# A hybrid encoder block on one core: the last token pair of the feed-forward's second half takes all its weights in one visit

## The chip, the core and the metric

The kernel runs on one core of a Trainium2 chip. A core has a matrix engine (TensorE, PE in the profile, with its weight loads shown apart as PEld), a vector engine (VectorE, DVE), a scalar engine (ScalarE, ACT), a general engine (GpSimd, POOL) and a queue that issues transfers (SyncE, SP). Data lie in SBUF; matmuls accumulate in eight PSUM banks of 128 x 512 floats. The metric is the time of one execution in device microseconds; a comparison uses the median of several.

## The reference

One layer of an encoder block, 2048 tokens and 16 meta tokens, width 1024, in float32:

```python
h = concatenate([meta, x], axis=1)
p = rms_norm(h, norm_mix_pre) @ w_in
mixed = concatenate([rg_lru(p), forgetting_attention(p), rwkv7(p)]) @ w_out
h = h + rms_norm(mixed, norm_mix_post)
f = causal_dwconv(rms_norm(h, norm_ffn_pre) @ ffn_up, ffn_conv)      # 1024 -> 2 x 2816
gate, val = split(f, 2)
f = (gelu(gate) * val) @ ffn_down                                    # 2816 -> 1024
h = h + rms_norm(f, norm_ffn_post)
return h[:, N_META:]
```

The change concerns the last four lines, above all `@ ffn_down` and the norm behind it, which end the kernel.

## The kernel before

**Numbers.** Every float32 operand of a matmul is split into a high part (`hi`, a copy on ACT, L1602) and a low part (`lo = x - hi`, on DVE, in places on POOL, L1603). One product is three matmuls, hi x hi, hi x lo and lo x hi (`mm3`, L172, L173, L174).

**The up stage** computes the first half of the feed-forward for blocks of 342 tokens in units j of the feature columns. It accumulates in banks `psu`. A unit's sums are combined on DVE, convolved (`conv`: an ACT scaling at L1736 into `uy` and two multiply-adds on DVE, L1738), put through the gelu and multiplied on POOL (L1744), and stored to the scratch `scr_ff` (L1745). Some units read their sum from an SBUF tile (`vb`), others straight from the PSUM bank.

**The down stage** (class `Down`) has 2048 tokens as eight token pairs of 256 tokens and 22 row blocks of `ffn_down`: ten weight pairs k = 0 to 9, and an eleventh, the rest. For each k a Strassen-like scheme takes seven products (`p1`, `p5`, `p7`, `p6`, `p2`, `p3`, `p4`) in place of eight, so 21 matmuls of 128 x 512. Its token operands come from `scr_ff` as `u` (256 KB, L1849), are summed by four POOL operations (L1856 to L1859) and split into `fo`. Its weight operands come as 256 KB loads `raw` (L1832) and are split into slots: nine kept ones (`qd`) and 26 of a ring (`dw`). Of the seven splits of a k, two have their low part on POOL, five on DVE. 35 slots hold five k. The rest is done without the scheme, 24 matmuls from weights `dwn`; three of its four sums share a bank with `p2`, `p3` and `p4`, the fourth has a bank `rb`.

As 35 slots do not hold ten k, the stage makes two rounds. `first` goes through the eight pairs with k = 0 to 4; each pair's seven banks are evacuated by ACT (L1888 to L1890) and DVE (L1891 to L1895, L1904) into four half rows `la`, `ra`, `lb`, `rb`, and stored to `scr_part`. Then `second` goes through the eight pairs with k = 5 to 9 and the rest; after the evacuation the stored part comes back (`pt`, 512 KB a row) and is added on POOL (L1901), the row is normalised (ACT squares L1516, the root L102 to L104, DVE L1525) and added to `h` (`hx`, loaded at L1920, L1526), and stored to the output (L1922). One pair has 105 matmuls in the first round and 129 in the second.

The operands of k = 0, and two of k = 1, are prepared in the last round of the up stage from unit j = 14 on (`DOWN_FROM`); the others follow when the down stage begins, the rest's weights with them. The operands of k = 5 to 9 are prepared when the last first visit no longer needs the slots of k = 0 to 4.

**What sets the order.** The kernel is written as one program; a scheduler puts it in an order for each engine, by dependences and due times. `issue_after(x)` keeps what is written in it behind x on the queues. Pools hand out buffers in turn (a tag has so many), and a tile waits until the last reader of its buffer is done. Each engine executes its own list in order.

## Time and profile before

| | us |
|---|---|
| median of 3 runs | 3065.51 (3058.34 to 3071.79) |
| the profiled execution | 3063.42 |
| its span | 3061.7 |
| last matmul of the up stage starts | 2592.17 |
| last matmul of the down stage starts | 3050.16 |

The mean granted clock of the profiled execution is 0.971. Times in a row are microseconds from the start of the span; `[3.57 <-DVE uy L1738]` behind a row says that the engine was idle for 3.57 us before it and that a DVE instruction of line 1738 that writes `uy` ended the idle time. In a table by stretches the numbers behind a stretch are its length, the busy time of each engine with the count of its instructions, the granted clock of PE, and the share and rate of the DMA engines. In a row of groups `xcount | busy, mean ns | idle before` stand for the number of instructions, their busy time in all and mean duration, and the idle time of the engine just before them with what ended it.

### The profile page before, as it was taken

Reading aid. Unit: us, or ns where it says so; the run is one execution under the profiler, and the core shown is the slowest. Engines: PE = TensorE matmul, PEld = TensorE weight load, DVE = VectorE, ACT = ScalarE, POOL = GpSimd, SP = SyncE. Lnnn points to the kernel's source line nnn. Section 1 sums busy time; section 2 is a strip of 40 time slices with the busy share of each in tenths; the row PEclk is TensorE's granted clock in tenths of the full one; section 3 lists DMA queues with packets and bytes.
Section 4 is the critical chain, followed back from the end, with each engine's and each line's share of the span. In section 5 each row is a group of like instructions: output and inputs, shape, how many; then the busy total and the mean of one; then the engine's idle time right before and its main releaser. Section 6 shows DMA issues by size and latency. Waiting matters only on the chain.

```text
span 3061.7 us, 52809 instructions
## 1 busy us (share of the span) xinstructions
PE 2910.2 (95%) x18694; PEld 2487.6 (81%) x18694; DVE 2057.7 (67%) x3934; ACT 1479.1 (48%) x2853; POOL 1365.7 (45%) x1599
## 2 busy tenths in 40 slices
PE   6998999999989999999999899999999999999998
PEld 6997898888876654566568899999999999787786
DVE  5268645656677785555636888888778777547766
ACT  4245332434346554454534656666566665324333
POOL 1001121122214556566843457445645544556765
PEclk8999999999989898999999999999999999999999
DMA  6776478466654347434336555566677765535454
GB/s 216 244 234 207 163 240 292 154 199 205 211 156 92 88 105 211 109 100 122 75 94 206 171 181 180 172 202 213 209 215 212 220 192 165 171 102 175 148 162 145
DMA packets 467750, 532.58 MB, mean 174 GB/s; under 512 B 85550, under 2 KB 355576, under 8 KB 465932
## 3 DMA queue, kind: packets, MB, share of 16 engines
q1 hardware_dynamic: 466716, 528.27, 56.5%
q8 instruction: 147, 2.41, 0.3%
q14 instruction: 119, 0.97, 0.1%
q0 software_dynamic: 768, 0.93, 0.1%
HBM read 369.11 MB, written 159.95 MB: 173 GB/s over the span
## 4 chain that ended last, share of the span: by engine, by line
PE 34%; DVE 5%; DMA 5%; POOL 3%; issue 3%; ACT 1%; SPq 0%; POOLq 0%; DVEq 0%; ACTq 0%
PE psu L172 8%; PE psu L173 8%; PE psu L174 8%; PE psd L172 2%; PE psd L173 2%; PE psd L174 2%; DMA u<-scr_ff 2%; DMA xt<-scr_h 1%; DVE uw L1603 1%; PE pswo L172 1%; PE pswo L174 1%; PE pswo L173 1%; DVE fo L1603 1%; DVE uy L1738 1%; POOL u L1858 1%
## 5 line engine op out<-in xcount | busy, mean ns | idle before, releaser
L172 PE MATMUL psu<-xo,uw 128*128 128x344 f32 x1848 | 590.8, 323 | 14.7 <-DVE vb L1787 6.9
L173 PE MATMUL psu<-xo,uw 128*128 128x344 f32 x1848 | 593.1, 321 | 0.0
L174 PE MATMUL psu<-xo,uw 128*128 128x344 f32 x1848 | 584.3, 320 | 1.5 <-DVE uw L1603 1.5
L172 PE MATMUL psp<-xh,wh 128*128 128x384 f32 (+2 forms) x1152 | 383.5, 333 | 4.5 <-ACT wh L166 3.0
L174 PE MATMUL psp<-xh,wl 128*128 128x384 f32 (+2 forms) x1152 | 379.5, 330 | 2.6 <-DMA wl<-scr_wk 2.5
L173 PE MATMUL psp<-xl,wh 128*128 128x384 f32 (+2 forms) x1152 | 379.3, 329 | 0.0
L1603 DVE TENSOR_TENSOR uw<-uq,uw 128x512 fp32r<-128x512 f32 x341 | 321.0, 947 | 65.1 <-ACT uw L1602 62.8
L172 PEld LDWEIGHTS psu<-xo,uw 128*128 128x128 f32 x1848 | 347.4, 189 | 19.2 <-DVE vb L1787 9.4
L174 PEld LDWEIGHTS psu<-xo,uw 128*128 128x128 f32 x1848 | 347.2, 189 | 2.4 <-DVE uw L1603 2.3
L173 PEld LDWEIGHTS psu<-xo,uw 128*128 128x128 f32 x1848 | 348.5, 189 | 0.1
L1602 ACT ACTIVATE uw<-uq 128x512 fp32r<-128x512 f32 x462 | 287.5, 627 | 107.5 <-PE psu L174 46.6
L686 ACT ACTIVATE p<-sc,bias 128x512 f32<-128x512 f32 (+4 forms) x352 | 197.0, 589 | 194.9 <-PE sc L682 162.1
L559 DVE TENSOR_REDUCE mc<-mx 128x1 f32<-128x512 f32 (+6 forms) x352 | 190.2, 564 | 114.1 <-PE mx L554 87.2
L1738 DVE SCALAR_TENSOR_TENSOR uy<-psu,ffn_cols,uy 128x342 f32<-128x342 f32 (+1 forms) x396 | 223.7, 567 | 62.3 <-ACT uy L1736 60.9
L1744 POOL TENSOR_TENSOR uy<-uy,uy 128x342 f32<-128x342 f32 (+1 forms) x132 | 140.0, 1061 | 252.7 <-DVE uy L1738 70.1
L725 POOL TENSOR_TENSOR acc<-acc,p 128x512 f32<-128x512 f32 (+3 forms) x208 | 221.7, 1068 | 53.1 <-DVE acc L725 23.9
L1603 POOL TENSOR_TENSOR uw<-uq,uw 128x512 fp32r<-128x512 f32 x121 | 177.6, 1468 | 148.0 <-ACT uw L1602 129.5
L172 PEld LDWEIGHTS psp<-xh,wh 128*128 128x128 f32 x1152 | 221.7, 192 | 11.6 <-issue 4.2
L174 PEld LDWEIGHTS psp<-xh,wl 128*128 128x128 f32 x1152 | 220.8, 192 | 12.0 <-issue 5.7
L173 PEld LDWEIGHTS psp<-xl,wh 128*128 128x128 f32 x1152 | 221.3, 192 | 7.5 <-issue 5.4
L1603 DVE TENSOR_TENSOR fo<-u,fo 128x896 fp32r<-128x896 f32 x88 | 109.0, 1240 | 118.8 <-ACT fo L1602 118.8
L1602 ACT ACTIVATE fo<-u 128x896 fp32r<-128x896 f32 x88 | 81.1, 922 | 200.9 <-POOL u L1859 103.8
(470 smaller groups left out, 6470.3 us busy)
## 6 DMA issues: line engine op xcount, KB each, us to landing
uq<-scr_us SPq DMA_DIRECT2D x220, 256.0 KB
uq<-in_ffn_up_dram SPq DMA_DIRECT2D x209, 256.0 KB
wl<-scr_wk SPq DMA_DIRECT2D x48, 512.0 KB
wh<-scr_wk SPq DMA_DIRECT2D x48, 512.0 KB
u<-scr_ff SPq DMA_DIRECT2D x88, 256.0 KB
scr_ff<-uy SPq DMA_DIRECT2D x110, 171.0 KB
raw<-in_w_in_dram SPq DMA_DIRECT2D x24, 512.0 KB
scr_wk<-wh SPq DMA_DIRECT2D x24, 512.0 KB
```

Source lines behind the costliest of these rows:

```text
L172: nc.tensor.matmul(out, ah, bh, start=first, stop=False, skip_group_check=more)
L173: nc.tensor.matmul(out, ah, bl, start=False, stop=False, skip_group_check=more)
L174: nc.tensor.matmul(out, al, bh, start=False, stop=last, skip_group_check=more)
L559: self.reduced = nc.vector.tensor_reduce(mc[:rows, i, ci : ci + 1], ps[:rows, : e - a], axis=AX.X, op=ALU.max)
L686: last = nc.scalar.activation(p[:rows, :w], ps[:rows, :w], AF.Exp, bias=bias[:rows, j : j + 1])
L725: eng.tensor_tensor(a, ps_[0][0][:rows, c0:n] if start and i == 1 else a, p[:rows, : n - c0], op=ALU.add)
L1602: core.nc.scalar.activation(hi, src, AF.Copy)
L1603: (eng or core.nc.vector).tensor_tensor(lo, src, hi, op=ALU.subtract)
L1738: stt(y[:, :n], src[:, i : n + i], cw[:, 44 * i + cc : 44 * i + cc + 1], y[:, :n], op0=ALU.mult, op1=ALU.add)
L1744: core.pooled = nc.gpsimd.tensor_tensor(v[:, :n], g[:, :n], v[:, :n], op=ALU.mult)
L1858: tt(s3, a0, b0, op=ALU.subtract)
```

## The change

- **The rounds.** `first` goes through seven pairs. The eighth takes k = 0 to 9 and the rest in one visit, stores no part, and is normalised and put out directly. `second` then goes through the other seven. The operands of k = 5 to 9 are written two k after the eighth pair's start (`ahead`, `DOWN_AHEAD`), behind its `u` loads, in one ring of 35 slots (25 `dw`, nine `qd` and a `kd` in the place of an earlier gain vector). The rest's weights are loaded and split in the fifth pair (`DOWN_REST`).
- **The stored parts.** They are loaded as four half rows of 256 KB (`fetch`, tag `dq`) in the visit before, and after the second k of a second visit (`DOWN_STORED`) three are added to the open banks of `p4`, `p2` and `p3` by DVE (L1924 of the changed kernel), while the fourth is copied to the `rb` bank by ACT. The matmuls that follow accumulate on top. The POOL additions of L1901 are gone.
- **The up stage's end.** The down operands begin at unit 13, three of k = 1 at unit 17. In the last unit the two sums that stayed in PSUM go to SBUF tiles (`u2`, `ga`), and a third bank is copied by ACT before its convolution. Splits of k = 2 and 3 are held behind the last convolution (`DOWN_HELD`, `ended`).
- **The end of a visit.** The rest goes in the order `p4`, `rb`, `p2`, `p3`, the evacuation in the order `lb`, `rb`, `la`, `ra`. `add_scaled` takes the place of `add_normed`: the half rows are multiplied by the gain (L1539) and then scaled and added in one DVE operation (L1543). Both `hx` rows are loaded together. In the last pair the products `p2`, `p3`, `p4` of k = 8 are kept to the end, and the output is stored by half rows.

The lines of the changed kernel are some 18 to 50 higher: the splits' L1603 is L1621 there, the side sums' L1856 to L1859 are L1886 to L1889, the evacuation's L1904 is L1948, and the convolution's L1738 is L1760.

Three places show how instructions move. First DVE at the end of the up stage, before: `uy` are the convolutions of the last unit, `dw` the low parts of down weights.

```order
L1790 TENSOR_TENSOR psu_28591<-psu_28591,ga_28525 128x344
L1603 TENSOR_TENSOR dw_28754<-raw_28752,dw_28754 128x512
L1603 TENSOR_TENSOR dw_28789<-raw_28787,dw_28789 128x512
L1603 TENSOR_TENSOR dw_28794<-raw_28792,dw_28794 128x512
L1738 SCALAR_TENSOR_TENSOR uy_28587<-vb_28540,ffn_cols,uy_28587 128x338
L1738 SCALAR_TENSOR_TENSOR uy_28605<-psu_28591,ffn_cols,uy_28605 128x342
L1738 SCALAR_TENSOR_TENSOR uy_28587<-vb_28540,ffn_cols,uy_28587 128x338
L1738 SCALAR_TENSOR_TENSOR uy_28624<-psu_28512,ffn_cols,uy_28624 128x342
```

The same place now:

```order
L1812 TENSOR_TENSOR vb_28553<-psu_28525,vb_28553 128x344
L1760 SCALAR_TENSOR_TENSOR uy_28600<-vb_28553,ffn_cols,uy_28600 128x338
L1760 SCALAR_TENSOR_TENSOR uy_28618<-ga_28538,ffn_cols,uy_28618 128x342
L1760 SCALAR_TENSOR_TENSOR uy_28600<-vb_28553,ffn_cols,uy_28600 128x338
L1760 SCALAR_TENSOR_TENSOR uy_28618<-ga_28538,ffn_cols,uy_28618 128x342
L1760 SCALAR_TENSOR_TENSOR uy_28639<-ga_28637,ffn_cols,uy_28639 128x342 x2
L1621 TENSOR_TENSOR dw_28748<-raw_28746,dw_28748 128x512
L1621 TENSOR_TENSOR dw_28753<-raw_28751,dw_28753 128x512
L1621 TENSOR_TENSOR fo_28793<-u_28787,fo_28793 128x896
```

The convolutions stand ahead of the splits, and read SBUF (`ga`, `vb`) where they read `psu`.

Second, POOL in the eighth pair, before: the four side sums of k = 3 end with the first row, those of k = 4 are `u_30183`.

```order
L1859 TENSOR_TENSOR u_30153<-u_30153 128x128
L1603 TENSOR_TENSOR qd_30233<-raw_30258,qd_30233 128x512
L1856 TENSOR_TENSOR u_30183<-u_30183 128x128
L1858 TENSOR_TENSOR u_30183<-u_30183 128x128
L1603 TENSOR_TENSOR qd_30233<-raw_30270,qd_30233 128x512
L1857 TENSOR_TENSOR u_30183<-u_30183 128x128
L1859 TENSOR_TENSOR u_30183<-u_30183 128x128
```

Now, with the side sums of k = 2 (`u_30141`) and k = 3 (`u_30199`):

```order
L1889 TENSOR_TENSOR u_30141<-u_30141 128x128
L1621 TENSOR_TENSOR qd_25384<-raw_30158,qd_25384 128x512
L1621 TENSOR_TENSOR qd_25384<-raw_30170,qd_25384 128x512
L1886 TENSOR_TENSOR u_30199<-u_30199 128x128
L1888 TENSOR_TENSOR u_30199<-u_30199 128x128
L1887 TENSOR_TENSOR u_30199<-u_30199 128x128
L1889 TENSOR_TENSOR u_30199<-u_30199 128x128
L1621 TENSOR_TENSOR kd_25385<-raw_30216,kd_25385 128x512
```

The first splits of the second five k stand one k earlier on POOL.

Third, DVE between two second visits, before, from the normalisation of one pair on; the `fo` are operands of the next pair.

```order
L1525 SCALAR_TENSOR_TENSOR ra_31315<-ra_31315,rs_5253_31338,g_fpost 128x512
L1603 TENSOR_TENSOR fo_31405<-u_31399,fo_31405 128x896
L102 TENSOR_SCALAR rs_5255_31351<-rs_5255_31351 128x1
L1526 TENSOR_TENSOR hx_31336<-hx_31336,la_31311 128x512
L1526 TENSOR_TENSOR hx_31336<-hx_31336,ra_31315 128x512
L104 RECIPROCAL rs_5255_31351<-rs_5255_31351 128x1
L1525 SCALAR_TENSOR_TENSOR lb_31313<-lb_31313,rs_5255_31351,g_fpost 128x512
L1525 SCALAR_TENSOR_TENSOR rb_31312<-rb_31312,rs_5255_31351,g_fpost 128x512
L1603 TENSOR_TENSOR fo_31435<-u_31429,fo_31435 128x896
L1526 TENSOR_TENSOR hx_31349<-hx_31349,lb_31313 128x512
L1526 TENSOR_TENSOR hx_31349<-hx_31349,rb_31312 128x512
L1603 TENSOR_TENSOR fo_31465<-u_31459,fo_31465 128x896
```

Now:

```order
L1543 SCALAR_TENSOR_TENSOR hx_30842<-lb_30827,rs_5183_30846,hx_30842 128x512
L1543 SCALAR_TENSOR_TENSOR hx_30842<-rb_30826,rs_5183_30846,hx_30842 128x512
L1621 TENSOR_TENSOR fo_30946<-u_30940,fo_30946 128x896
L104 RECIPROCAL rs_5184_30857<-rs_5184_30857 128x1
L1543 SCALAR_TENSOR_TENSOR hx_30844<-la_30825,rs_5184_30857,hx_30844 128x512
L1543 SCALAR_TENSOR_TENSOR hx_30844<-ra_30829,rs_5184_30857,hx_30844 128x512
L1924 TENSOR_TENSOR psd_30872<-psd_30872,pt_30762 128x512
L1924 TENSOR_TENSOR psd_30873<-psd_30873,pt_30764 128x512
L1924 TENSOR_TENSOR psd_30874<-psd_30874,pt_30758 128x512
L1621 TENSOR_TENSOR fo_30976<-u_30970,fo_30976 128x896
```

The additions into the open banks stand between the third and the fourth `fo` of the next pair, behind the whole normalisation of the last one.

The diff's core:

```diff
+def add_scaled(core, pool, halves, gain, x, junk):
...
+    for y, acc in zip(halves, sums):
+        nc.scalar.activation(junk, y, AF.Square, accum_out=acc)
+    for c, y in enumerate(halves):
+        nc.vector.tensor_tensor(y, y, gain[:, 512 * c : 512 * c + 512], op=ALU.mult)
+    r1 = rstd_root(core, v, sums, D)
+    for c, y in enumerate(halves):
+        xc = x[:, 512 * c : 512 * c + 512]
+        nc.vector.scalar_tensor_tensor(xc, y, r1, xc, op0=ALU.mult, op1=ALU.add)
+        yield xc
...
-DOWN_SLOTS = 5, 13, 8
-DOWN_FROM = 14
+DOWN_SLOTS = 5, 7, 1, 2, 10
+DOWN_FROM = 13, 17
+DOWN_HELD = 2, 4
+DOWN_AHEAD = 2
+DOWN_FETCH, DOWN_STORED = 2, 1
+DOWN_REST = 4
...
             elif name == "p3":
-                tt(ps, ps, u2, op=ALU.add)
-                gb = conv(ps, 0, j, n[1])
+                sum_ = ps if more else u2
+                tt(sum_, ps, u2, op=ALU.add)
+                gb = conv(sum_, 0, j, n[1])
...
-                va = conv(ps, 1, j, n[0])
+                src = ps
+                if not more:
+                    src = s("ga")
+                    nc.scalar.activation(src, ps, AF.Copy)
+                va = conv(src, 1, j, n[0])
...
+            products(k, side, slice(0, 4))
+            kept.append((k, side, slice(4, None)))
+            while kept and not (rest and following is None and k == ks[-2]):
+                products(*kept.pop(0))
+            if stored and i == DOWN_STORED:
+                for name, half in zip(("p4", "rb", "p2", "p3"), self.parts):
+                    if name == "rb":
+                        nc.scalar.activation(ps[name][:], half[:], AF.Copy)
+                    else:
+                        tt(ps[name][:], ps[name][:], half[:], op=ALU.add)
+            if following is not None and k == ks[-DOWN_FETCH]:
+                with core.tc.issue_after(self.loaded.ins):
+                    self.parts = self.fetch(following)
...
-        for i, row in enumerate(((lb, rb), (la, ra)) if rest else ()):
-            t0 = P * (2 * pair + i)
-            pt = self.spool.tile([P, D], F32, tag="hx", name=core.n("pt"))
-            nc.sync.dma_start(pt[:], self.scr["part"][t0 : t0 + P, :])
-            for c, y in enumerate(row):
-                nc.gpsimd.tensor_tensor(y, y, pt[:, 512 * c : 512 * c + 512], op=ALU.add)
-        for y, name in ((la, "p2"), (ra, "p3"), (lb, "p4"), (rb, "rb")):
+        for y, name in ((lb, "p4"), (rb, "rb"), (la, "p2"), (ra, "p3")):
...
+        steps.second(pairs - 1, range(DOWN_PAIRS), weights, ahead, rest, False, 0)
+        for pair in range(pairs - 1):
+            following = pair + 1 if pair < pairs - 2 else None
+            steps.second(pair, range(DOWN_CUT, DOWN_PAIRS), weights, lambda i: None, rest, True, following)
```

176 lines of the change are left out of this document (109 added, 67 removed).

## The prediction

> **What bounds the kernel now.** I read the share of the engines first, then a table of busy time in stretches around the feed-forward's second half, then PE's waits there, then the order of PE's instructions inside the two worst stretches. The columns of a stretch are its length, and busy us and count of PE, PEld, DVE, ACT and POOL, the granted clock, the DMA share and GB/s; the table of the psum tile `psd` alone has PE, PEld, DVE and ACT.
>
> ```profile
> PE 2910.2 (95%) x18694; PEld 2487.6 (81%) x18694; DVE 2057.7 (67%) x3934; ACT 1479.1 (48%) x2853; POOL 1365.7 (45%) x1599
> 2300.00:2570.00 270.00, 269.03 (x1702) 268.65 (x1701) 209.67 (x338) 166.72 (x336) 121.67 (x98) 1.00 0.67 197
> 2600.00:2630.00 30.00, 27.83 (x103) 20.63 (x103) 20.34 (x20) 17.73 (x28) 16.71 (x19) 0.91 0.75 257
> 2750.00:2780.00 30.00, 30.00 (x131) 24.46 (x130) 16.01 (x20) 7.30 (x9) 15.29 (x24) 1.00 0.32 108
> 2780.00:2810.00 30.00, 25.41 (x97) 19.43 (x96) 27.54 (x26) 21.96 (x37) 26.86 (x26) 0.89 0.75 245
> 2810.00:2840.00 30.00, 28.76 (x125) 23.13 (x124) 23.21 (x25) 10.34 (x17) 20.87 (x24) 0.99 0.40 130
> 2900.00:2930.00 30.00, 29.47 (x129) 23.72 (x128) 20.89 (x27) 9.96 (x19) 20.67 (x25) 1.00 0.49 158
> 3050.00:3062.00 12.00, 0.55 (x3) 0.12 (x1) 7.19 (x15) 2.97 (x10) 1.36 (x2) 0.61 0.36 134
> ```
> ```profile
> 2592.00:2600.00 8.00, 2.75 (x7) 1.67 (x8) 0.00 (x0) 0.00 (x0) 0.71 0.57 166
> ```
> ```profile
> L1888 ACT ACTIVATE la<-psd x5: 598/598/602, 2675.0 to 2771.6; 128x512 f32<-128x512 f32 x5
> L1888 ACT ACTIVATE la<-psd x7: 597/598/598, 2859.8 to 3042.3; 128x512 f32<-128x512 f32 x7
> ```
>
> PE is the bound, so the change is worth only the time that PE loses. The evacuation `la<-psd` comes once per token pair and is my pace-maker. Four intervals of the first visits give (2771.6-2675.0)/4 = 24.15 us for 105 matmuls, 0.230 us each. Against that pace a stretch is worth its length minus 0.230 us times its matmuls. The up stage (2300 to 2570) has PE busy 269 of 270 us. The steady first visits have 131 matmuls in 30 us, no loss. The losses are three, and a tail:
> - The step from up to down. After 2592.33 (row below) seven matmuls stand in the 7.67 us to 2600, a loss of 6.1, and 103 in the next 30 us, a loss of 6.3: together 12.4 us.
> - The step from first to second visits: 97 matmuls in 2780 to 2810 lose 7.7, 125 in the next 30 us lose 1.2: 8.9 us.
> - The second visits: six intervals give (3042.3-2859.8)/6 = 30.42 us for 129 matmuls, whose pace would be 29.67: 0.75 us per pair.
> - The tail from PE's last matmul to the end of the span.
>
> ```profile
> PE psd L172 <- ACT fo L1602: 6.1, 8, 2.8
> PE psd L172 <- DVE uy L1738: 4.9, 2, 3.6
> PE psd L174 <- DVE fo L1603: 3.7, 4, 1.3
> ```
> ```profile
> 2592.33 0.39 PE L172 MATMUL psd<-qd,fo 128*128 128x512 f32 x1
> 2596.76 0.77 PE L172 MATMUL psd<-qd,fo 128*128 128x512 f32 x1 [3.57 <-DVE uy L1738]
> 2599.72 0.76 PE L172 MATMUL psd<-qd,fo 128*128 128x512 f32 x1 [1.34 <-DVE uy L1738]
> 2602.42 0.63 PE L172 MATMUL psd<-qd,fo 128*128 128x512 f32 x1
> 2602.85 0.63 PE L173 MATMUL psd<-qd,fo 128*128 128x512 f32 x1
> ```
>
> The waits (total, times, longest) name what PE waited for: at the first step the last convolution `uy` on DVE, which still reads PSUM banks that the down stage wants; elsewhere the token operand `fo`. After the 3.57 us stop matmuls start 0.43 us apart (2602.42, 2602.85), about half pace, so a long stop is paid a second time.
>
> **The change, part by part.** All sums are against the profiled execution (3063.42 us, span 3061.7); it lies 2.1 us under the median 3065.51 of the three runs, so a gain is taken from the median in the end.
>
> (a) More first slots. Three more operands are split during the up stage, with their loads on SP, copies on ACT and subtractions on DVE or POOL. The last 270 us of the up stage leave DVE 60 us free and ACT 103, and PE never starves there: 0, with bounds 0 and 1 (one DVE split lying in PE's way).
>
> (b) The last up unit gives its PSUM up early: its sums go to SBUF, one copy on ACT replaces the convolution's direct read, and splits of k = 2 and 3 are held behind the last convolution. DVE runs the convolutions first (order rows in the section on the change). That removes the two waits on `uy`, 4.9 us, and with them the slow matmuls: in 2600 to 2612 there are about 4 us of those.
>
> ```profile
> 2600.00:2612.00 12.00, 11.14 (x34) 7.99 (x34) 0.00 (x0) 0.00 (x0) 0.77 0.87 306
> L1603 DVE TENSOR_TENSOR dw<-raw,dw 128x512 fp32r<-128x512 f32 x18 | 15.9, 923 | 3.1 <-ACT dw L1602 3.1
> L1603 DVE TENSOR_TENSOR fo<-u,fo 128x896 fp32r<-128x896 f32 x6 | 8.3, 1379 | 7.9 <-ACT fo L1602 7.9
> ```
>
> The 34 matmuls lose 12-34x0.230 = 4.2 us. What is late next is DVE: of each k's seven splits it does five, 5x0.923+1.379 = 6.0 us per k against PE's 21x0.230 = 4.83. Four operands of k = 1 and all of k = 2 to 4 are left, so DVE falls back 1.2 us for each of three k, about 3.5 us, while pair 1's work on k = 0 can fill some of it. The held splits wait behind the stores of the last `uy` on SP's and DVE's queues; behind them stand the `fo` of pair 0. Loss after: 3.5, with ends 1.5 (only the last k late) and 7 (all four k late and one slow spell). The loads and splits of the last two weight rows move from this place to the fifth pair, where a stretch like 2750 to 2780 has DVE free for 14 of 30 us: 0 there. I take 3.5, since the DVE rows give it: 12.4 becomes 3.5, -8.9, between -5.4 and -10.9.
>
> (c) The eighth pair takes ten k in one visit, in place of a first visit, its stores, a reload and a second visit. Its 35 splits for k = 5 to 9 go where the first-to-second step has them now, one k earlier in POOL's order. Here POOL decides, and it was busy 26.86 of 30 us:
>
> ```profile
> L1603 POOL TENSOR_TENSOR dw<-raw,dw 128x512 fp32r<-128x512 f32 x8 | 13.7, 1721 | 2.3 <-ACT dw L1602 2.3
> L1858 POOL TENSOR_TENSOR u<-u 128x128 f32<-128x128 f32 x7 | 7.1, 1013 | 0.0
> L1857 POOL TENSOR_TENSOR u<-u 128x128 f32<-128x128 f32 x7 | 5.4, 770 | 0.0
> L1859 POOL TENSOR_TENSOR u<-u 128x128 f32<-128x128 f32 x7 | 5.4, 769 | 0.5
> L1856 POOL TENSOR_TENSOR u<-u 128x128 f32<-128x128 f32 x7 | 5.0, 715 | 6.8 <-DMA u<-scr_ff 6.5 <-issue 0.3
> ```
>
> Per k: two splits 3.44 plus four side sums 3.27, 6.7 us against PE's 4.83. Over five k POOL falls back 9.4 us; it can be about one k (4.83) ahead when it begins. So PE still loses 9.4-4.8 = 4.6 us. Today it loses 8.9, with its evacuation and stores in the same stretch and a slow spell. The evacuation in the middle of that pair, its stores and their reload fall away. Now -4.3; ends +3 (POOL has no lead, and a slow spell of 2.5 us, less than the 4.2 of (b): 9.4+2.5 = 11.9 lost) and -7.
>
> (d) Stored parts in the second visits. The four POOL additions L1901 go; four loads of 256 KB stand behind a `u` load on SP; three DVE additions into open banks and one ACT copy come in, behind the second k of the next pair.
>
> ```profile
> L1901 POOL TENSOR_TENSOR la<-la,pt 128x512 f32<-128x512 f32 x4 | 7.0, 1740 | 0.0
> L1901 POOL TENSOR_TENSOR rb<-rb,pt 128x512 f32<-128x512 f32 x4 | 5.2, 1296 | 0.0
> L1856 POOL TENSOR_TENSOR u<-u 128x128 f32<-128x128 f32 x20 | 12.4, 622 | 37.8 <-DMA u<-scr_ff 33.6 <-DVE la L1525 3.2 <-DVE rb L1893 0.6
> L1602 ACT ACTIVATE fo<-u 128x896 fp32r<-128x896 f32 x20 | 19.0, 950 | 38.1 <-POOL u L1859 38.1
> L1784 DVE TENSOR_TENSOR psu<-psu,u 128x344 f32<-128x344 f32 x3 | 1.6, 518 | 1.3 <-PE psu L174 1.3
> L1904 DVE TENSOR_TENSOR la<-la,psd 128x512 f32<-128x512 f32 x5 | 3.4, 674 | 0.0
> L1526 DVE TENSOR_TENSOR hx<-hx,la 128x512 f32<-128x512 f32 x4 | 3.5, 882 | 0.0
> ```
> ```profile
> 3056.97 0.69 DVE L1526 TENSOR_TENSOR hx<-hx,rb 128x512 f32<-128x512 f32 x1
> ```
>
> Today POOL's side sums wait for L1525 behind the additions, `fo` waits for POOL, PE for `fo`: that is the 0.75 us per pair, and it goes. The price of the new addition is bounded by L1784, the one DVE addition into PSUM in this trace: 0.518 x 512/344 = 0.77 us, and from below by L1904, 0.67. I take 0.77, the same write. What may be late is DVE: from the last matmul of a pair it has eight evacuations and gain products (8x0.67), two `fo` (2x1.38), four scale-and-adds (4x0.69 as at 3056.97, or 4x0.88 beside POOL), and then the additions to p4 and p2 (2x0.77): 12.4 to 13.2 us, less one evacuation that it does before that matmul. PE comes to p2 of the third k after 2x4.83 plus 12 matmuls, 12.4 us. So it just fits or just doesn't; I put 0.3 us per pair, with ends 0 and 1.5 (0.88 for each of DVE's operations without PSUM, and the roots' small ones between them). Over seven pairs: 7x(0.3-0.75) = -3.2; ends -5.3 and +5.3.
>
> By the Trainium skill, page "GPSIMD Engine Reference", section "Key points", GpSimd's SBUF interfaces are contended by VectorE operations with two SBUF inputs. L1904 (one input from PSUM) against L1526 (two from SBUF) agrees, 674 and 882 ns; by the rule, with POOL's additions gone, DVE's two-input operations would come back toward 0.69, the 0.3 would be 0, and the sum 2.1 us lower.
>
> (e) The tail.
>
> ```profile
> 3050.16 0.39 PE L174 MATMUL psd<-dwn,fo 128*128 128x512 f32 x1
> 3054.95 3.07 SPq L1922 DMA_DIRECT2D out_dram<-hx  x2
> ```
>
> From 3050.55 to 3061.7 are 11.1 us: DVE to 3057.66, then the store of 512 KB, 4.0. The new normalisation multiplies by the gain before the sum of squares is there, so two DVE operations (1.4 us) leave the path, while the last stored half is 256 KB; POOL's additions leave it too, but DVE's order hides them. ACT's squares still come one after another. The other order of the rest's products and the products of k = 8 kept back in the last pair move matmuls without adding any: 0, since what follows on DVE is the same work in the same number of steps. I take -1.3, ends 0 and -2.
>
> Sum: 0-8.9-4.3-3.2-1.3 = -17.7 us. That is 3045.7 for the profiled execution, 3047.8 for the median: 3048.
>
> **Rivals.** First, the eighth pair stays as dear as the step it replaces (POOL 6.7 per k with no lead): (c) is +3 in place of -4.3 and the sum -10.4, 3055. For it: POOL's 26.86 of 30 us, and DVE's 27.54; against: the evacuation and stores that leave this stretch.
>
> Second, on the other side: the additions in open banks come late. `fo` of the fourth k stands behind them on DVE, and PE behind both. The place is p4 or p2 of the third k in each of seven pairs. For it: my sum has no slack; against: DVE is busy only 20.89 of 30 us. Its point: without (d)'s own gain the rest is -14.5 us, 2.1 per pair, so a stop of 2.1+0.75 us per pair brings the time back to 3065.5. A stop of 3.5 is followed by a slow spell as at 2596.76, which costs some 4.2: then 7x(3.5+4.2-0.75)-14.5 = +34, 3100; stops of 1.5, as bounded, give 3056. The Trainium skill ("TensorE: Matmul & The Clock Gate", part 1 on the HAM clock gate) puts the halving after about 3.4 us without work, in a window that runs freely. This trace agrees for the 3.57 us stop, but it also shows
>
> ```profile
> 2802.27 0.50 PE L172 MATMUL psd<-qd,fo 128*128 128x512 f32 x1 [2.81 <-ACT fo L1602]
> 2804.79 1.22 PE L174 MATMUL psd<-qd,fo 128*128 128x512 f32 x2 [1.31 <-DVE fo L1603]
> 2806.23 0.63 PE L173 MATMUL psd<-qd,fo 128*128 128x512 f32 x1
> ```
>
> where stops of 2.81 and 1.31 us close together were enough, so I price a stop from some 3 us on with a slow spell.
>
> Third, everything fits: (b) reaches -10.9, (c) -7, (d) -5.3, (e) -2, which is -25: 3040.
>
> **How the numbers follow.** The forecast has 0.52, the first rival 0.15, the second 0.18, the third 0.15. About 0.5% (15.3 us) is what a measurement of this kernel can tell from no change. The forecast's own range, 3041 to 3057, lies for four fifths below 3050.2: 0.43 faster and 0.09 same; the third rival is faster. The first rival is same. The second splits: 0.07 same (short stops), 0.11 slower than 3080.8. So faster 0.58, same 0.31, slower 0.11. The range 3036 to 3066 leaves out the second rival's long stops and the ends' far tails, less than 2 in 10.
>
> **What will show it.** (b): no wait of PE on `uy` over 1 us, no granted clock under 0.9 in the 20 us after the last up matmul, and some 140 matmuls or more in the 36 us after it. (c): the eighth pair's ten k in 53 us or less. (d): `la<-psd` of the second visits 30.0 us apart, and PE's waits on the additions under 0.5 us. (e): 9.8 us from PE's last matmul to the end. I am wrong if PE waits for DVE at p4 or p2 in each second visit, if POOL's lead in the eighth pair is gone, or if the up stage itself, which the change barely touches, gets longer.

## The result

The changed kernel takes 3044.18 us (median of six runs, 3038.31 to 3050.67), the kernel before 3063.36 us (median of six, 3058.34 to 3071.79): a ratio of 0.994, 95% interval 0.9928 to 0.9952, so 19.2 us or 0.6% faster. Ratios are of runs in the chip's fast state; the one slow run on record (4047.54 us at a granted clock of 0.641, of the kernel timed last below) is left out of them. The forecast was 3048 with a range of 3036 to 3066. The time was right; its parts were only partly right, and two of them for wrong reasons.

The profiled execution of the changed kernel has a span of 3042.5 us (3044.26 us in all), 19.2 us under that of the kernel before. The first question is where in the program these 19.2 us lie. The first matmul of the up stage tells (group of the matmuls `psu` of line 172, durations min/median/max, first and last start), first of the kernel before, then of the changed kernel:

```profile
L172 PE MATMUL psu<-xo,uw x1848: 314/321/656, 1682.0 to 2591.9; 128*128 128x344 f32 x185
```
```profile
L172 PE MATMUL psu<-xo,uw x1848: 315/321/653, 1675.0 to 2586.4; 128*128 128x344 f32 x185
```

7.0 us were won before the up stage begins, where both programs run the same instructions, in the same order but for a few matmuls that changed places. In the fourteen profiles of this study that start lies anywhere between 1674.5 and 1696.4 us: it is scatter. The up stage itself takes 909.9 and 911.4 us, from the first to the last start of these rows. What the change did is read from the down stage, from its first matmul to the end of the span: 469.4 us before, 455.6 now, -13.8 us. That measure is steady: a kernel that was profiled twice (below) gave 451.0 and 451.2. All comparisons below are made on it.

PE's stretches in the changed kernel (columns as before, the first number behind the stretch its length):

```profile
2590.00:2600.00 10.00, 9.17 (x39) 6.71 (x37) 6.08 (x7) 6.02 (x11) 4.02 (x4) 1.00 0.92 310
2600.00:2630.00 30.00, 26.96 (x105) 18.99 (x106) 23.58 (x26) 14.48 (x24) 22.49 (x26) 1.00 0.60 205
2850.00:2880.00 30.00, 30.00 (x132) 24.52 (x131) 20.47 (x31) 10.64 (x21) 12.47 (x21) 1.00 0.47 158
3030.00:3043.00 13.00, 3.03 (x14) 2.15 (x12) 8.57 (x17) 3.48 (x10) 0.00 (x0) 0.80 0.22 81
```

The pace-maker `la<-psd`, now line 1938, with the first matmul of the down stage ahead of it:

```profile
L172 PE MATMUL psd<-qd,fo x45: 390/394/502, 2586.9 to 2696.7; 128*128 128x512 f32 x45
```
```profile
L1938 ACT ACTIVATE la<-psd x2: 579/590/600, 2614.3 to 2639.8; 128x512 f32<-128x512 f32 x2
```
```profile
L1938 ACT ACTIVATE la<-psd x3: 598/599/601, 2760.6 to 2848.3; 128x512 f32<-128x512 f32 x3
```
```profile
L1938 ACT ACTIVATE la<-psd x7: 598/599/601, 2848.3 to 3026.2; 128x512 f32<-128x512 f32 x7
```

And PE's waits from 2560 us on:

```profile
PE psd L172 <- ACT fo L1620: 5.5, 3, 3.3
PE psd L173 <- DVE dw L1621: 1.8, 4, 0.7
PE psu L172 <- DVE vb L1812: 0.6, 1, 0.6
PE psd L172 <- ACT dw L1620: 0.6, 1, 0.6
```

Four stages follow from these rows. "Step up to down" runs from the first down matmul to the second `la<-psd`, 199 matmuls in both kernels. "Eighth pair" runs from the seventh first visit's `la<-psd` to that of the second of the stored visits, less 0.230 us for each matmul that starts in it. The matmuls have to be counted, since `la<-psd` doesn't stand at the same place of a visit in all kernels: 339 start there in the kernel before and 345 in the changed one, and 35 and 29 follow the last `la<-psd`. These are the two stretches, before and now (their counts take in one matmul that is under way at the edge):

```profile
2771.65:2859.82 88.17, 82.33 (x340) 64.90 (x339) 71.12 (x79) 42.88 (x71) 63.07 (x68) 0.96 0.57 188
```
```profile
2760.60:2848.26 87.66, 82.78 (x346) 66.55 (x345) 62.34 (x74) 42.06 (x70) 54.67 (x67) 0.96 0.68 228
```

The expectations below were written with 339 matmuls for every kernel (78.0 us), which makes a loss of 9.7 us of the changed kernel's 8.3. The pace of the second visits is the mean of the last six intervals, and the tail runs from the last matmul's start to the end of the span.

| | before | changed | difference |
|---|---|---|---|
| step up to down, us | 58.5 | 52.9 | -5.6 |
| loss at the eighth pair | 10.2 | 8.3 | -1.9 |
| second visits, apart | 30.42 | 29.65 | 6 x -0.77 = -4.6 |
| tail | 11.5 | 9.9 | -1.6 |
| down stage to the end | 469.4 | 455.6 | -13.8 |

The 0.1 us that the rows leave is rounding and the visits between.

The second visits lose nothing any more: 132 matmuls in 30 us, PE busy 30.00. The waits on `uy` are gone, the granted clock is 1.00 in both stretches behind the up stage. What is left lies at two places. In 2600 to 2630 PE does 105 matmuls where 130 would fit. In the eighth pair stands one long stop with a slow spell behind it; PE, a stretch, and POOL ahead of the stop:

```profile
2786.07 0.80 PE L172 MATMUL psd<-dw,fo 128*128 128x512 f32 x1 [3.35 <-ACT fo L1620]
```
```profile
2786.00:2793.00 7.00, 6.93 (x18) 5.47 (x19) 5.61 (x7) 4.93 (x10) 5.55 (x7) 0.56 0.80 265
```
```profile
2778.18 1.69 POOL L1621 TENSOR_TENSOR kd<-raw,kd 128x512 fp32r<-128x512 f32 x1 [1.58 <-DMA raw<-in_ffn_down_dram]
2779.83 1.75 POOL L1621 TENSOR_TENSOR dw<-raw,dw 128x512 fp32r<-128x512 f32 x1
2781.54 0.91 POOL L1886 TENSOR_TENSOR u<-u 128x128 f32<-128x128 f32 x1
2782.42 0.90 POOL L1888 TENSOR_TENSOR u<-u 128x128 f32<-128x128 f32 x1
```

POOL waits 1.58 us for a weight load, then does two splits, and only then the side sums from which `fo` of the next k is made. PE stands for 3.35 us, and in the 7 us from 2786 on it does 18 matmuls at a granted clock of 0.56: 7.0 - 18 x 0.230 = 2.9 us more. With the second stop (1.53 us) that is 7.8 of the 8.3 us.

The tail, from the last matmul on:

```profile
3032.64 0.40 PE L174 MATMUL psd<-dwn,fo 128*128 128x512 f32 x1
...
3036.47 3.03 SPq L1987 DMA_DIRECT2D out_dram<-hx  x4
...
3038.40 0.75 DVE L1543 SCALAR_TENSOR_TENSOR hx<-ra,rs,hx 128x512 f32<-128x512 f32 x1
```

DVE ends 6.5 us after the last matmul's start, where it was 7.5, and the last store lands 3.4 us later, where it was 4.0.

### The profile page after: what moved, and what is told of

It reads as the page before. It is cut to its first block, busy times and chain, and to the rows that moved or that the text cites. A ratio compares the mean times of both kernels' runs of the same rounds, so it can differ in the third digit from the quotient of the medians.

```text
span 3042.5 us, 52754 instructions
## 1 busy us (share of the span) xinstructions
PE 2901.8 (95%) x18694; PEld 2486.7 (82%) x18694; DVE 2043.7 (67%) x3947; ACT 1480.9 (49%) x2858; POOL 1309.2 (43%) x1567
## 3 DMA queue, kind: packets, MB, share of 16 engines
q1 hardware_dynamic: 468156, 526.17, 56.6%
## 5 line engine op out<-in xcount | busy, mean ns | idle before, releaser
L1621 DVE TENSOR_TENSOR uw<-uq,uw 128x512 fp32r<-128x512 f32 x341 | 316.9, 936 | 67.9 <-ACT uw L1620 65.8
L1760 DVE SCALAR_TENSOR_TENSOR uy<-psu,ffn_cols,uy 128x342 f32<-128x342 f32 (+1 forms) x390 | 220.2, 566 | 57.4 <-ACT uy L1758 55.7
L1621 POOL TENSOR_TENSOR uw<-uq,uw 128x512 fp32r<-128x512 f32 x121 | 180.9, 1495 | 148.4 <-ACT uw L1620 130.5
L174 PEld LDWEIGHTS psp<-xh,wl 128*128 128x128 f32 x1152 | 221.3, 192 | 11.5 <-issue 6.0
L1621 DVE TENSOR_TENSOR fo<-u,fo 128x896 fp32r<-128x896 f32 x88 | 100.1, 1138 | 132.7 <-ACT fo L1620 132.2
```

Of the source, the lines that this page charges most:

```text
L174: nc.tensor.matmul(out, al, bh, start=False, stop=last, skip_group_check=more)
L1621: (eng or core.nc.vector).tensor_tensor(lo, src, hi, op=ALU.subtract)
L1760: core.conved = stt(y[:, :n], src[:, i : n + i], cw[:, 44 * i + cc : 44 * i + cc + 1], y[:, :n], op0=ALU.mult, op1=ALU.add)
```

## The experiments

Each kernel is the changed kernel or the kernel before with the edit shown. All times are of the down stage, by the stages of the table above; a table at the end has them together. Four of the kernels were also timed against the kernel before: ratios of 0.9949 (sums stay in PSUM), 0.9972 (two rounds), 0.9960 (parts on POOL, ahead) and 0.9958 (old normalisation). Their down stages alone would give 0.9956, 0.9972, 0.9964 and 0.9961, each inside the interval of its ratio. The others, the last apart, were run once.

**The banks given up early (undone).**

```diff
-DOWN_HELD = 2, 4
+DOWN_HELD = 0, 0
...
-                sum_ = ps if more else u2
+                sum_ = ps
...
-                sum_ = ps if more else ga
+                sum_ = ps
...
-                if not more:
-                    src = s("ga")
-                    nc.scalar.activation(src, ps, AF.Copy)
```

> The changed kernel with one part undone: in the last up unit the sums stay in PSUM and are convolved from there, and the splits of k = 2 and 3 are not held behind the last convolution; the earlier start of the down operands stays. My theory (the banks were what PE waited for): PE waits for the convolution again, 3 to 5 us, and a slow spell follows; from the last up matmul to the first la<-psd about 33 us, against 27.4 in the changed kernel and 35.7 before; the time 4 to 6 us over the changed kernel's. Rival (the order on DVE and the earlier slots did it, the banks not): 27 to 28.5 us there, and no difference in time over 1 us.

The first down matmul, the first two `la<-psd`, and the wait on `uy`:

```profile
L172 PE MATMUL psd<-qd,fo x36: 390/395/498, 2597.3 to 2683.3; 128*128 128x512 f32 x36
```
```profile
L1935 ACT ACTIVATE la<-psd x2: 580/590/600, 2625.0 to 2650.5; 128x512 f32<-128x512 f32 x2
```
```profile
PE psd L172 <- DVE uy L1760: 0.4, 1, 0.4
```

27.7 us to the first `la<-psd` against 27.4, and 0.2 us in the whole down stage. My theory fell: the convolutions may read PSUM to the end, and PE waits 0.4 us for them. In this kernel too the scheduler has the convolutions ahead of the weight splits on DVE. In the kernel before three splits stand ahead of them (2.17 us from 2590.90 on), and two more ahead of the last one:

```profile
2590.90 2.17 DVE L1603 TENSOR_TENSOR dw<-raw,dw 128x512 fp32r<-128x512 f32 x3 [0.19 <-ACT dw L1602]
```

**Fewer first slots, and the rest's weights early.** Two kernels: none of k = 1 is prepared in the up stage; or the rest's two weight rows are loaded in the first pair.

```diff
-DOWN_FROM = 13, 17
+DOWN_FROM = 14,
```

> The changed kernel with the down operands prepared from unit 14 on and none of k = 1 in the up stage (three more operands are left for the step from up to down). Theory A (transfers bound that step: DMA share 0.92 in its first 10 us, and ACT waits for raw loads): 3 x 256 KB at some 300 GB/s, so the first la<-psd comes 2.5 to 3 us later than 27.4 us after the last up matmul. Theory B (DVE's order alone made the step shorter): within 0.5 us of 27.4.

```diff
-DOWN_REST = 4
+DOWN_REST = 0
```

> The changed kernel with the rest's two weight rows (1 MB of loads, two ACT copies, two DVE subtractions of 128x1024) in the first pair in place of the fifth. Theory A (transfers and DVE bound the step): the first and the second la<-psd together come 2.5 to 5 us later. Theory B (order alone): within 0.5 us.

First down matmul and first two `la<-psd`, of the kernel with fewer slots and of that with the rest early:

```profile
L172 PE MATMUL psd<-qd,fo x41: 390/392/404, 2590.9 to 2699.8; 128*128 128x512 f32 x41
```
```profile
L1938 ACT ACTIVATE la<-psd x2: 582/590/598, 2620.2 to 2646.2; 128x512 f32<-128x512 f32 x2
```
```profile
L172 PE MATMUL psd<-qd,fo x37: 390/394/497, 2593.2 to 2699.9; 128*128 128x512 f32 x37
```
```profile
L1938 ACT ACTIVATE la<-psd x2: 580/590/599, 2623.5 to 2649.1; 128x512 f32<-128x512 f32 x2
```

The second `la<-psd` comes 55.3 and 55.9 us after the first matmul, against 52.9: 2.3 and 2.9 us later (the first one 1.9 and 2.9). So work taken out of this step is worth time there.

The 2.9 us belong to the change: 1 MB of loads, two copies and two subtractions went to the fifth pair. In the kernel before they lie in this step; the first of the two subtractions:

```profile
2602.66 1.23 DVE L167 TENSOR_TENSOR dwn<-raw,dwn 128x1024 fp32r<-128x1024 f32 x1 [0.52 <-ACT dwn L166]
```

The 2.3 us do not: the three operands of k = 1 that this run takes away are not three more than before. When the first down matmul starts, the kernel before has split twelve weight operands (seven of k = 0, two some 10 us ahead of that matmul and three in the last 1.4 us), the changed kernel ten, this run seven. So about half of the 5.6 us is the rest's work moved away. What makes up the other 2.7 is not shown. The order on DVE is the likeliest, since no kernel with the convolutions ahead of the splits has a wait on `uy` over 0.4 us, but no run undoes it.

**Two rounds of eight pairs.**

```diff
-        for pair in range(pairs - 1):
+        for pair in range(pairs):
             def ahead(i): ...
...
-        steps.second(pairs - 1, range(DOWN_PAIRS), weights, ahead, rest, False, 0)
-        for pair in range(pairs - 1):
+        for pair in range(pairs):
```

In it the first stored visit loads its parts in its own first k, and the operands of k = 5 to 9 are written where they are first used, not two k ahead.

> The changed kernel with eight first visits and eight second visits, all with stored parts added in open banks. My theory after the result (the one visit moved the loss and did not remove it, since POOL, DVE and the transfers have the same 35 splits to do in the same 50 us): from the la<-psd of the seventh first visit to that of the second second visit the loss against pace stays within 2 us of the changed kernel's 9.7 us. Rival (the one visit is worth the 4.3 us that I predicted): the loss is 13 to 14 us.

The four `la<-psd` of the step, of this kernel and, for comparison, of the kernel before:

```profile
L1940 ACT ACTIVATE la<-psd x4: 579/598/600, 2771.2 to 2863.9; 128x512 f32<-128x512 f32 x4
```
```profile
L1888 ACT ACTIVATE la<-psd x4: 581/597/598, 2771.6 to 2859.8; 128x512 f32<-128x512 f32 x4
```

92.7 us for 345 matmuls (79.3) is a loss of 13.3 us, 5.0 more than with the one visit, as the rival said and I no longer believed. The kernel before loses only 10.2 us with two rounds, though. Of the 5.0, 1.6 lie in the interval from the first to the second stored visit (33.3 us for 138 matmuls, 31.7 at pace), where this kernel has a late load of parts that neither of the others has. The other 3.4 are the price of two rounds and of the later place of the operands together.

**One visit alone, on the kernel before.**

```diff
-        for pair in range(pairs):
+        for pair in range(pairs - 1):
             steps.first(pair, ks[0], weights)
...
+        steps.second(pairs - 1, range(DOWN_PAIRS), weights, last, False)
-        for pair in range(pairs):
+        for pair in range(pairs - 1):
             steps.second(pair, ks[1], weights, last)
```

> The kernel before with one difference: the eighth pair takes ten k in one visit, prepared as the scheduler likes, without loads ahead. Theory A (one visit is worth what the two-round variant of the changed kernel lost, 5 us): from the seventh first visit's la<-psd to the second second visit's the loss against pace falls from 10 to about 5 us. Theory B (the splits' work sets that step whatever the visits): it stays within 2 us of 10.

```profile
L1888 ACT ACTIVATE la<-psd x3: 597/598/599, 2770.9 to 2856.9; 128x512 f32<-128x512 f32 x3
```

86.0 us for 339 matmuls, a loss of 8.1: 2.1 us better than before, nearer to theory B, and about what the changed kernel gains there (1.9). Its later visits are 30.7 us apart, so that the down stage as a whole gains 0.3 us (469.1); why they got slower is open. Alone the visit is worth next to nothing.

**The stored parts on POOL, loaded ahead.** The three additions and the copy into banks go; the parts still come a visit ahead.

```diff
+        parts = self.parts if stored else None
...
-            if stored and i == DOWN_STORED:
+            if False:
...
+        if stored:
+            for y, half in zip((lb, rb, la, ra), parts):
+                nc.gpsimd.tensor_tensor(y, y, half[:], op=ALU.add)
```

> The changed kernel with the stored parts added on POOL behind the evacuation, as before; the parts still come as four loads one visit ahead. My theory: the second visits go back to about 30.4 us apart, against 29.65, 5 us in all over seven pairs, with PE waiting for fo. Rival (the earlier loads and the other order of the evacuation did it, not the engine of the addition): they stay below 29.9 us apart.

**The stored parts on POOL, loaded late,** as rows into the two buffers `hx`, which the rows of h use too; the additions into banks and the loads ahead go:

```diff
...
+        for i, row in enumerate(((lb, rb), (la, ra)) if stored else ()):
+            t0 = P * (2 * pair + i)
+            pt = self.spool.tile([P, D], F32, tag="hx", name=core.n("pt"))
+            nc.sync.dma_start(pt[:], self.scr["part"][t0 : t0 + P, :])
+            for c, y in enumerate(row):
+                nc.gpsimd.tensor_tensor(y, y, pt[:, 512 * c : 512 * c + 512], op=ALU.add)
```

> The changed kernel with the stored parts loaded as before: behind the evacuation, as rows of 512 KB, into the two row buffers that the loads of h use as well, and added on POOL. Theory A (what the second visits gained lies in SP's queue: the loads of h wait for POOL to free the row buffers, with u loads queued behind them): the second visits go back to 30.2 us apart or more, against 29.86 where POOL adds parts that were loaded ahead, and SP waits for POOL again. Theory B (the new evacuation and normalisation order gave the gain): they stay at 29.9 or less.

The seven last `la<-psd` with parts loaded ahead, then with parts loaded late:

```profile
L1939 ACT ACTIVATE la<-psd x7: 599/599/599, 2868.3 to 3047.3; 128x512 f32<-128x512 f32 x7
```
```profile
L1938 ACT ACTIVATE la<-psd x7: 598/598/601, 2859.0 to 3039.5; 128x512 f32<-128x512 f32 x7
```

29.83 and 30.08 us apart. So the 0.77 us per visit fall into three: 30.42 to 30.08 with the parts as before, but the new order of rest, evacuation and normalisation; 30.08 to 29.83 with parts loaded ahead; 29.83 to 29.65 with DVE in place of POOL. This is one way through the three, with one profile each, and within a profile on POOL the intervals differ by up to 0.5 us, so the parts are rough. The first takes several edits together, the common load of both `hx` rows among them. Neither theory held whole. What SP waits for shows why loads ahead help: over four visits, the kernel before, that with late parts, and the changed one.

```profile
SPq L1920 <- POOL ra L1901: 36.3, 4, 9.2
```
```profile
SPq L1973 <- POOL ra L1951: 36.2, 4, 9.2
```
```profile
SPq L1877 <- DVE fo L1621: 90.5, 22, 6.5
...
SPq L1967 <- DMA out_dram<-hx: 4.4, 4, 1.5
```

A load of `hx` waits up to 9.2 us for POOL to have used up the parts in its buffer, and the next `u` load comes only behind it; SP in the kernel before:

```profile
2887.57 2.15 SPq L1849 DMA_DIRECT2D u<-scr_ff  x2
2899.03 0.33 SPq L1920 DMA_DIRECT2D hx<-scr_h  x1
2899.45 0.39 SPq L1849 DMA_DIRECT2D u<-scr_ff  x1
```

In the changed kernel SP waits for `fo`, that is, for PE's own pace. The kernel with late parts has the same waits as the kernel before and is still 0.34 us per visit faster, so the waits alone are not the 0.77; taking them away, by loads ahead, is worth 0.25 us there. With POOL adding ahead-loaded parts, the tail too is 2.2 us longer (12.1 us).

**The parts in the raw ring, on the kernel before.** One difference: half rows in the ring of the weight loads.

```diff
-            pt = self.spool.tile([P, D], F32, tag="hx", name=core.n("pt"))
-            nc.sync.dma_start(pt[:], self.scr["part"][t0 : t0 + P, :])
+            for c in range(2):
+                pt = self.rpool.tile([P, 512], F32, tag="dq", name=core.n("pt"))
+                nc.sync.dma_start(pt[:], self.scr["part"][t0 : t0 + P, 512 * c : 512 * c + 512])
...
```

> The kernel before with one difference: the stored parts are loaded as half rows into the raw ring in place of the two row buffers that the loads of h use as well; POOL still adds them. Theory A (in the kernel before, the loads of h on SP wait until POOL has used up the row buffers, and the u loads queue behind them): the second visits go from 30.4 us apart to 29.9 or less. Theory B (POOL's additions ahead of the side sums are the delay, as I predicted): they stay at 30.3 us or more.

The visits are 30.66 us apart, no better. The edit didn't take the wait away, as SP's waits over four visits show:

```profile
SPq L1901 <- POOL la L1904: 31.3, 5, 7.2
```

Now the load of the parts itself waits for POOL, at the same place of the queue. So this run tells nothing against the queue, and nothing for it.

**The old normalisation.**

```diff
-            for c, done in enumerate(add_scaled(core, self.spool, halves, self.gain, hx[i], junk)):
-                if following is None:
-                    nc.sync.dma_start(self.out[t0 : t0 + P, 512 * c : 512 * c + 512], done)
-            if following is not None:
-                nc.sync.dma_start(self.out[t0 : t0 + P, :], hx[i][:])
+            add_normed(core, self.spool, halves, P, self.gain, hx[i], [junk] * 2)
+            nc.sync.dma_start(self.out[t0 : t0 + P, :], hx[i][:])
```

> The changed kernel with the normalisation and the whole-row stores of before. My theory: only the tail changes, PE's last matmul to the end 11 us against 9.5; the second visits stay 29.65 us apart, since DVE does the same number of steps ahead of the additions into the banks. Rival (the new normalisation is what lets the additions come in time): the second visits take 30 us or more, and PE waits for DVE at the additions.

The tail is 10.3 us against 9.9, not 11; the visits are 29.71 us apart on the mean (29.8 at first, 29.65 later). The whole down stage is 1.7 us longer. Both theories claimed too much.

**The eighth pair: order or amount of POOL's work.** First, the side sums of the next k written ahead of the weights of the second five; and, at another place, the gain vector's load of 512 KB moved from the step up to down to the fourth pair.

```diff
-            side = self.side(k, pair)
+            side = early.pop(k) if k in early else self.side(k, pair)
             weights(k)
+            if soon and k != ks[-1]:
+                early[k + 1] = self.side(k + 1, pair)
             ahead(i)
...
-            if pair == 1:
+            if pair == 3:
                 gain = ...
-                nc.sync.dma_start(g_fpost[:], gain)
+                with tc.issue_after(steps.loaded.ins):
+                    nc.sync.dma_start(g_fpost[:], gain)
```

> The changed kernel with two edits at different places: in the eighth pair the side sums and fo of the next k are written ahead of the weights of the second five k, so that POOL does them first; and the gain vector's load of 512 KB moves from the step from up to down to the fourth pair. Theory A (in the eighth pair the 3.35 us stop comes from side sums that stand behind POOL splits which wait for their loads; the step from up to down is bound by transfers): the eighth pair's loss falls from 9.7 to 5 us or less, the first two la<-psd come 1 to 2 us sooner. Theory B (POOL's and DVE's work in all bounds the eighth pair, whatever the order): its loss stays within 1.5 us of 9.7.

Then one POOL split per k for k = 5 to 9 in place of two:

```diff
-        split(core, hl[:, 0], hl[:, 1], t, core.nc.gpsimd if i in DOWN_POOLED else None)
+        split(core, hl[:, 0], hl[:, 1], t, core.nc.gpsimd if i in DOWN_POOLED[: 1 + (k < DOWN_CUT)] else None)
```

> The changed kernel with one POOL split per k in place of two for k = 5 to 9, the other on DVE. Theory A (POOL is the bound in the eighth pair, 6.7 us per k of work against 4.83): POOL has 1.7 us per k less, and the loss falls from 9.7 to 5 us or less. Theory B (DVE is as full, so that the work only moves): the loss stays within 2 us of 9.7 or grows.

The three `la<-psd` and PE's waits in the eighth pair, with the side sums ahead:

```profile
L1941 ACT ACTIVATE la<-psd x3: 598/599/599, 2761.4 to 2849.0; 128x512 f32<-128x512 f32 x3
```
```profile
PE psd L172 <- ACT fo L1620: 4.5, 4, 2.3
```

and with one POOL split:

```profile
L1938 ACT ACTIVATE la<-psd x3: 598/602/602, 2764.0 to 2847.4; 128x512 f32<-128x512 f32 x3
```
```profile
PE psd L172 <- ACT fo L1620: 3.2, 2, 1.6
```
```profile
2786.00:2796.00 10.00, 8.42 (x36) 6.51 (x36) 9.53 (x11) 7.67 (x13) 8.73 (x9) 1.00 0.86 281
2796.00:2806.00 10.00, 8.38 (x37) 6.51 (x36) 9.52 (x10) 6.18 (x10) 9.51 (x10) 1.00 0.92 318
```

The order alone does nothing: four stops of 4.5 us in all in place of two of 4.9, and a loss of 87.6 - 79.4 = 8.2 us against 8.3. The amount does: the loss is 83.4 - 79.4 = 4.0 us, 4.3 less, where theory A asked for a fall of 4.7. The stops are 1.7 us shorter in all, and no slow spell follows them, of 1.5 and 1.6 us (the clock is 1.00 in each stretch), which saves the 2.9 us from above. Now POOL, DVE and the transfers are all nearly full there (9.5 of 10 us each, DMA share 0.92). The step up to down became 2.0 us longer with the gain's load moved, not shorter; PE waited there for DVE and POOL splits up to 1.8 us. So transfers alone don't bound that step; why it lost is open.

**The version with one POOL split, timed.**

> The same kernel as the one with one POOL split per k for k = 5 to 9, timed in rounds. From its stages (451.0 us from the last up matmul to the end, against 455.6 of the changed kernel and 469.4 before) it should be 18.4 us faster than the kernel before, a ratio of 0.994, and 4.6 us faster than the changed kernel; what lies ahead of the down stage, the same instructions in all these kernels, moved by up to 20 us from run to run, so the ratio may come out between 0.990 and 0.997. The stage itself should again be 451.0 within 0.5.

A ratio of 0.9935 to the kernel before, interval 0.9922 to 0.9948 (the medians, 3052.24 and 3068.19, give 0.9948, its upper end). The down stage took 451.2 us, as expected. By this measure it is 4.5 us faster than the changed kernel and 18.2 faster than the kernel before. By total times alone the two changed kernels can't be told apart.

| us | step up to down | loss, eighth pair | visits apart | tail | down stage to end |
|---|---|---|---|---|---|
| before | 58.5 | 10.2 | 30.42 | 11.5 | 469.4 |
| changed | 52.9 | 8.3 | 29.65 | 9.9 | 455.6 |
| sums stay in PSUM | 53.2 | 8.2 | 29.66 | 9.9 | 455.8 |
| fewer first slots | 55.3 | 8.3 | 29.64 | 9.9 | 457.9 |
| rest early | 55.9 | 7.6 | 29.66 | 9.9 | 457.9 |
| two rounds | 54.5 | 13.3 | 29.65 | 10.0 | 460.7 |
| parts on POOL, ahead | 52.8 | 7.9 | 29.83 | 12.1 | 458.4 |
| parts on POOL, late | 53.3 | 11.2 | 30.08 | 12.0 | 463.5 |
| old normalisation | 53.2 | 9.0 | 29.71 | 10.3 | 457.3 |
| side sums ahead, gain late | 54.9 | 8.2 | 29.66 | 9.9 | 457.5 |
| one POOL split | 52.6 | 4.0 | 29.66 | 9.9 | 451.0 |
| one visit alone, on before | 58.5 | 8.1 | 30.74 | 11.5 | 469.1 |
| parts in ring, on before | 59.9 | 12.0 | 30.66 | 11.1 | 474.3 |

The step has 199 matmuls in all of them but "two rounds" (208; less those nine it is 52.4 us). The eighth pair has 345, with parts added on POOL and in the kernel before 339, with parts in the ring 342.

## Why the prediction came out as it did

The sum was -17.7 us. The medians say -19.2, the down stage -13.8. The interval of the ratio ends at -14.7, a little beyond what the stages show; the rest I put down to the scatter ahead of the up stage, which is larger than that and which no run here removes. Of the profiled execution's 19.2 us, 5.4 lie ahead of the down stage. That the time came out within 4 us of 3048 is so in part luck; the 13.8 us that the change made lie 3.9 us under the sum.

- **(a) and (b), the step up to down, -8.9 predicted, -5.6 measured.** The waits on `uy` went, and the slow matmuls behind them, as argued. What failed is the cause and the loss that I left. I read these waits as waits for PSUM banks, to be ended by copies to SBUF; with the sums back in PSUM they do not return (0.4 us). The step's loss was 12.7 us (58.5 - 199 x 0.230) and is 7.2, where I left 3.5: 125 matmuls in the 36 us, not 140. My DVE rate of 6.0 us per k was too fast a start: in 2590 to 2600 DVE is busy 6.08 of 10 us, since it waits for ACT, and ACT in part for raw loads, at a DMA share of 0.92. The rest's weights moved away, priced at 0, are worth 2.9 us: I had costed them where they went and not where they left. And (a) had no ground, since the changed kernel enters the down stage with ten operands split, and the kernel before with twelve; the change adds one slot (`kd`), not three, and fills them earlier.
- **(c), the eighth pair, -4.3 predicted, -1.9 measured.** POOL as the bound was right: with one split per k taken off it (1.7 of the surplus of 1.9 us), 4.3 us go. The lead of 4.83 us that I gave POOL was wrong: from 2766.5 to 2778.2 it is idle for 4.8 us, since its first splits and side sums wait for loads and for ACT, and the stop of 3.35 us was followed by a slow spell. The ten k, for which the sign was 53 us or less, took about 56.6 (210 x 0.230 + 8.3). The loss of 8.3 us lies halfway between the forecast's 4.6 and the first rival's 11.9; the rival's mechanism, no lead and a slow spell, is what the rows show.
- **(d), the second visits, -3.2 predicted, -4.6 measured.** The additions in open banks are never late, so the rival on the other side has no place. The addition takes 683 ns, not 770 (L1784, from which I took the 770, was not the only addition into PSUM before: L1790 is another, at 0.52 us), and `fo` became shorter; DVE's rows of four visits, before and now:

```profile
L1603 DVE TENSOR_TENSOR fo<-u,fo 128x896 fp32r<-128x896 f32 x21 | 29.6, 1411 | 14.6 <-ACT fo L1602 14.6
```
```profile
L1621 DVE TENSOR_TENSOR fo<-u,fo 128x896 fp32r<-128x896 f32 x21 | 24.5, 1168 | 18.8 <-ACT fo L1620 18.5
L1924 DVE TENSOR_TENSOR psd<-psd,pt 128x512 f32<-128x512 f32 x12 | 7.5, 683 | 0.0
```

  The prediction weighed the Trainium skill's rule of the page "GPSIMD Engine Reference", "Key points", that POOL contends with VectorE operations of two SBUF inputs: by it DVE gains time and nothing is lost at the additions. That is what the trace shows, `fo` 1411 to 1168 ns with POOL busy 12.5 (row of 2850 to 2880) in place of 20.7 of 30 us, and the loss 0. With POOL's additions put back, `fo` took 1294 ns (parts loaded ahead) and 1235 ns (late). But the cause that I named for the old 0.75 us, POOL's additions ahead of the side sums, explains a part only, 0.18 us in the one way through that was measured; the loads ahead (0.25) and the new order of rest, evacuation and normalisation (0.34) are the larger part.
- **(e), the tail, -1.3 predicted, -1.6 measured.** The size was right, the share not: undoing the new normalisation and the half-row stores costs 0.4 us only. Putting POOL's additions back costs 2.2 us, more than the whole gain, though I had costed them at nothing because DVE's order would hide them. How much of the 1.6 they are isn't shown, since they meet another order there than in the kernel before.

So the total came out right because gains too large in (b), by 3.3 us, and (c), by 2.4, met one too small in (d), by 1.4, and the scatter of the early stages did the rest.

## What to carry to other kernels

When work is moved away from a place where PE starves, price it at the place that it leaves as well as where it goes (the rest's weights: 2.9 us there, 0 by the forecast). A wait that names a convolution or a bank tells who came last, not what would have to go: undoing the one suspected part showed here in one run that it was not needed. When a stretch is measured between two marks, count the work between them: the mark here had moved by six matmuls, 1.4 us. A load that waits for a buffer held up the loads behind it on SP; loading such data a visit ahead, into buffers that no slower engine empties late, was worth 0.25 us per visit here.

## What the runs showed of the hardware

A stop of PE need not be long to be followed by half pace: 3.35 us gave a granted clock of 0.56 over the next 7 us, but in the kernel with the side sums ahead the clock was 0.83 in the stretch of a stop of 2.26 us, while stops of 1.5 and 1.6 us left it at 1.00. In the down stages of all fourteen profiles there are 19 stops of 2.1 us or more (2.14 to 3.70); behind each, six to thirteen of the next 25 matmuls start some 0.43 us apart, in place of 0.23. Behind a stop of 1.2 to 1.8 us this was seen only where others lay close to it. The stop and its stretch:

```profile
2797.78 0.50 PE L172 MATMUL psd<-qd,fo 128*128 128x512 f32 x1 [2.26 <-ACT fo L1620]
```
```profile
2792.00:2802.00 10.00, 7.74 (x28) 5.83 (x27) 7.33 (x8) 5.04 (x9) 9.84 (x11) 0.83 0.86 286
```
The Trainium skill ("TensorE: Matmul & The Clock Gate", part 1) puts the slow clock behind an idle window of about 3.4 us. The runs don't agree: a stop of 2.14 us is shorter than such a window and was followed by half pace too.

The time at which the up stage begins, after the same instructions, varied over 22 us from profile to profile (1674.5 to 1696.4), while the down stage of the one kernel that was profiled twice took 451.0 and 451.2 us.
